# Weights as one hi/lo buffer at three offsets, and four operand arrangements in the FFN's way up

## The chip, the cores and the metric

The kernel runs on one core of one Trainium2 chip. The metric is device time in microseconds (us). The kernel before took 1268.47 us, the median of 3 runs (1268.17 to 1268.96). TensorE does the matmuls, ScalarE (ACT) and VectorE (DVE) the elementwise work, and DMA queues bring the weights in.

## The reference

A causal decoder trunk of two layers on 512 tokens of width 1024, all in float32. Cut to what matters:

```python
x = x + even_mixer(rmsnorm(x, norm_mix[0]), ...)   # gated linear attention + differential attention
x = x + conv_ffn(rmsnorm(x, norm_ffn[0]), ...)
x = x + odd_mixer(rmsnorm(x, norm_mix[1]), ...)    # three groups of dilated windowed attention
x = x + conv_ffn(rmsnorm(x, norm_ffn[1]), ...)

def conv_ffn(h, w_up, conv_w, conv_b, w_down):     # w_up: 1024 x 5632, w_down: 2816 x 1024
    u = causal_depthwise_conv3(h @ w_up, conv_w) + conv_b
    gate, val = jnp.split(u, 2, axis=-1)
    return (jax.nn.silu(gate) * val) @ w_down
```

## The kernel before

The residual `xT` stays on chip, features on the partitions and the 512 tokens along the free axis, in 8 chunks of 128 features. Every dense product takes float32r operands. Each float32 operand is split as `hi` + `lo`, and a product is three matmuls: hi*hi, lo*hi and hi*lo, added in one PSUM bank of 512 float32 columns. A matmul has a stationary operand (128x128, brought in by its own LDWEIGHTS) and a moving operand, whose columns stream past it.

**Weights.** `weight_slabs()` lists 208 pieces ("slabs") in the order of their use. Most are 128 x 1024 values, 8 row chunks of 128 columns in the FFN's way up. `load_next()` (lines 160 to 176) brings one in: a DMA from SyncE's queue into `raw`, an ACT copy that rounds it into `hi` (line 171), and a DVE subtraction that leaves `lo` (line 174). `raw`, `hi` and `lo` are tiles of 1088 elements (4352 bytes) on each partition with 3 copies each, so slab i uses copy i mod 3. `slab()` hands out slab i and first issues the loads up to slab i+2, so the slab being converted is used two slabs later and goes into the copy that slab i-1 has just left.

**Products.** `tok_gemm` (line 304) is for the mixers' input projections: the tokens `hhi`/`hlo` are stationary and the weights move. For the second and third attention group of layer 1 the 128 stationary tokens are every fourth one (`v1`, line 793), so that an LDWEIGHTS reads every fourth float32 of a row. `feat_gemm` (line 320) is for the mixers' output projections: weights stationary, activations moving. The FFN works on 22 hidden chunks in groups of 8, 8 and 6. `up(j)` (lines 700 to 708) computes one 128-feature chunk of the way up: 8 row chunks times 3 matmuls, weights stationary, all 512 tokens of `hhi`/`hlo` moving, into one bank. It runs for the gate half and the value half of each chunk, 44 times in each layer. `gate` (line 724) does the convolution, SiLU and product on DVE and ACT and splits the result into `ghi`/`glo`. `down` (line 740) is the way down: weights stationary, `ghi`/`glo` moving (line 747).

**Order.** TensorE runs in the order in which the code emits its work. In the mixers small attention products are put between the dense ones at estimated times. The FFN is emitted straight, way up and way down by groups, and the first chunk of the next group's way up goes ahead of a way down. The other engines are scheduled by the framework, which puts a wait where tiles are reused.

Of the kernel before, what the change touches and what calls it, by code (L numbers as in the profile page):

```python
"""Two-layer hybrid trunk (GLA + differential attention, dilated attention, conv-FFN) on one core.

The residual stays on chip feature-major.  Every dense product runs on TensorE with float32r operands: each
float32 operand w is split exactly as w = hi + lo (hi rounded to float32r, lo the rest) and the product is
hi*hi + hi*lo + lo*hi in float32 PSUM.  The attention products are plain float32.
"""
# [11 lines left out]
F32R = mybir.dt.float32r  # L18
# [6 lines left out]
P = 128  # L25
S = 512
D = 1024
# [7 lines left out]
# columns of the packed constant array  # L35
C_ID, C_LT, C_SM = 0, P, 2 * P
C_KEEP = C_SM + 8
# the rest is kept only as long as it is needed
# [29 lines left out]
# groups of the FFN's hidden chunks that stay on chip between the way up and the way down  # L68
# [3 lines left out]

def weight_slabs():
    """The weights' pieces in the order of their use: (array, layer, first row, chunks of 128 rows, first column,
    columns).  On chip a piece has a row of each chunk on every partition."""
    slabs = []

    def tok(w, c0, n):
        nk = 2 if n == 512 else 4
        slabs.extend((w, 0, k * P, nk, c0, n) for k in range(0, DC, nk))  # L80

    def ffn(i):
        for gi, (f0, n) in enumerate(GROUPS):
            # the next group's first chunk goes before this group's way down
            for j in range(f0 + (gi > 0), f0 + n + (gi < 2)):
                slabs.extend(("ffn_w_up", i, 0, DC, half + j * P, P) for half in (0, DFF))
            slabs.extend(("ffn_w_down", i, f0 * P, n, c * P, P) for c in range(DC))

    for c0, n in ((2576, 512), (1552, 512), (2064, 512), (0, 512), (1280, 272), (512, 512), (1024, 256)):
        tok("ev_w_in", c0, n)  # L90
    for r0 in (512, 0):
        slabs.extend(("ev_w_out", 0, r0, 4, c0, 256) for c0 in range(0, D, 256))
    ffn(0)
    for g, kind in ((0, 0), (0, 1), (1, 0), (1, 1), (2, 0), (2, 1), (1, 2), (2, 2), (0, 2)):
        tok("od_w_in", g * 1536 + kind * 512, 512)
    slabs.extend(("od_w_out", 0, 0, 4, c0, 256) for c0 in range(0, D, 256))
    ffn(1)
    return slabs


def lay_out(a):
    """The kernel's arrays: the inputs in the order in which the chip reads them."""
    def cols(v):
        """(..., 128 n) with 128 consecutive entries on the partitions."""
# [5 lines left out]
    weights = [a[w][i, r0:r0 + nk * P, c0:c0 + n].reshape(nk, P, n).transpose(1, 0, 2).ravel()  # L110
               for w, i, r0, nk, c0, n in weight_slabs()]
# [11 lines left out]
def trunk_kernel(ctx: ExitStack, tc: tile.TileContext, x, weights, params, lqks, w_a2, consts, out):  # L123
# [18 lines left out]
    # ---------------------------------------------------------------- constants and small parameters  # L142
# [7 lines left out]
    # ---------------------------------------------------------------- weight slabs  # L150
# [3 lines left out]
    for _, _, _, a, _, b in weight_slabs():  # L154
        slabs.append((weights[off:off + P * a * b].rearrange("(p n) -> p n", p=P), a, b))
        off += P * a * b

    loaded = []

    def load_next():  # L160
        src, a, b = slabs[len(loaded)]
        n = a * b
        raw = wp.tile([P, SLAB], F32, name="raw", bufs=3)
        hi = wp.tile([P, SLAB], F32R, name="hi", bufs=3)
        lo = wp.tile([P, SLAB], F32R, name="lo", bufs=3)
        # the first product waits for its weights: they come in halves
# [8 lines left out]
        v = [t[:, :n].rearrange("p (a b) -> p a b", a=a) for t in (hi, lo)]  # L175
        loaded.append(v)

# [9 lines left out]
    # ---------------------------------------------------------------- residual, h, norms  # L187
# [4 lines left out]
    def split(hi, lo, src, gain):  # L192
        """hi + lo = src * gain, each in float32r."""
# [7 lines left out]
    def rsqrt(dst, ss, scale, work=None):  # L201
        """dst = 1 / sqrt(ss * scale + EPS): a table start and a Newton step."""
# [23 lines left out]
    def rstd_of(cols):  # L226
        """1/rms of tokens, one column of 128 tokens for each entry of cols (views of sqacc)."""
# [8 lines left out]
    def rstd_rows():  # L236
        """1/rms of tokens as a row for every partition."""
# [17 lines left out]
    def masked(out, sc, mask, nm):  # L255
        """out = -(sc + mask), nm its row minimum: minus the row maximum of the masked scores."""
# [3 lines left out]
    # ---------------------------------------------------------------- TensorE's order  # L260
    # TensorE runs in emission order in the mixers.  The dense products are the background; a piece of attention
    # work is put into the stream once its estimated time has come, so that it finds its operands ready.
# [28 lines left out]
    def tok_gemm(n, lhs, evict, before=None):  # L291
        """Token-major projection block: n columns, lhs(h, t) the stationary tokens."""
# [20 lines left out]
    def feat_gemm(nk, ncol, rhi, rlo, evict):  # L313
        """Feature-major product: one slab of nk row chunks and ncol columns, moving rhi/rlo[k]."""
# [13 lines left out]
    # ================================================================ layer 0 mixer  # L328
# [3 lines left out]
    def norm_scale(src, nh, r=None):  # L332
        """1/rms of each of nh heads of src along the free axis; r scales src's rows first."""
# [20 lines left out]
    def qk_evict(dst, gain, nh, r, tag, then=None):  # L354
        """Normalise heads, lay them feature-major into dst."""
# [29 lines left out]
    with tc.tile_pool(name="m0", bufs=1) as m0, tc.tile_pool(name="t0", bufs=2) as t0:  # L385
# [18 lines left out]
        def prepare_params():  # L404
            """Parameters that the first products do not need."""
            # gains that enter scores: both norms' gains and the score scale on the query side
# [12 lines left out]
        # ---- start: a slab of weights for every two chunks of the residual  # L419
# [32 lines left out]
        def head_norm(src, n, dst_hi, dst_lo, gain, gate, tag):  # L452
            """RMS-norm each 128-wide head of src (SBUF, token-major), gate, and lay it feature-major as hi + lo."""
# [10 lines left out]
        # ---- differential attention, one (query tile, head) after the other  # L464
        # estimated waits, in us
# [60 lines left out]
        # ---- gated linear attention, one 128-token tile after the other  # L526
# [38 lines left out]
        def decay3(t, y2):  # L565
            """exp of a tile's summed decays and of its first chunk's, by head, the 64 rows twice."""
# [59 lines left out]
        def when_landed(fn):  # L626
            """After the values and all gates have been produced."""
# [47 lines left out]
        def late(t, ps):  # L675
            # the residual's norm is known only by then
# [20 lines left out]
    # ================================================================ FFN  # L697
    def ffn(i, done):
        with tc.tile_pool(name=f"f{i}", bufs=2) as fp:
            def up(j):  # L700
                whi, wlo = slab()
                ps = bank()
                for kc in range(DC):
                    for m, (w, r) in enumerate(((whi, hhi), (wlo, hhi), (whi, hlo))):
                        T.matmul(ps, w[:, kc], r[:, kc], start=(kc == 0 and m == 0),  # L705
# [34 lines left out]
            def down(gi):  # L740
# [15 lines left out]
                # the last group's last chunk comes late: it enters four accumulators after all the others  # L756
# [9 lines left out]
                for c in range(first, DC):  # L766
                    w = slab()
                    # the kernel's last chunk goes out in halves
# [23 lines left out]
    # ================================================================ layer 1 mixer  # L792
# [3 lines left out]
    # groups 1 and 2 take their tokens by residue modulo 4; dilation 16 is a mask within a residue's tile  # L796
# [11 lines left out]
    with tc.tile_pool(name="m1", bufs=1) as m1:  # L808
# [8 lines left out]
        # probabilities: a block of 128 keys for each (head, query tile)  # L817
# [168 lines left out]
```

## Time and profile before

| | before |
|---|---|
| median of 3 runs | 1268.47 us |
| span of the profiled execution | 1266.7 us |
| PE busy | 1254.2 us (99%) |
| DVE busy | 766.1 us (60%) |
| ACT busy | 541.2 us (43%) |
| weights and inputs read | 110.37 MB |

The profiled execution is one run of the program. Its own time is its span, from the first to the last instruction; the median of the timed runs is 1.8 us longer than that span. PE is TensorE's matmul side and PEld its weight loads, which overlap the matmuls. A matmul's record is longer (about 0.39 us) than the distance to the next matmul's start, since they are pipelined; the pace of a stream is read from the starts, or from the chain of work that ended last, which counts each piece of time once.

### The profile page before, as it was taken

How to read it: one execution, taken by the hardware profiler on the slowest of the kernel's cores; microseconds unless marked ns; L12 is line 12 of the kernel's file. 1: busy time of each engine (PE TensorE's matmuls, PEld its weight loads, DVE VectorE, ACT ScalarE, POOL GpSimd, SP SyncE). 2: the span in 40 equal slices, each digit the busy share in tenths (PEclk: the TensorE clock that was granted, in tenths of full speed). 3: DMA queues.
4: the chain of work that ended last, by engine and by line, in shares of the span. 5: the costliest groups of instructions: out<-in, count | busy, mean ns of one | idle time of the engine just before them, and what ended most of it. 6: DMA issues, size and time to landing. Idle time of an engine off the chain costs nothing.

```text
span 1266.7 us, 15144 instructions
## 1 busy us (share of the span) xinstructions
PE 1254.2 (99%) x5878; PEld 1053.7 (83%) x5878; DVE 766.1 (60%) x1409; ACT 541.2 (43%) x895; POOL 5.7 (0%) x13
## 2 busy tenths in 40 slices
PE   8999999999999999999999999999999999999998
PEld 6878688888888888888889999988888888888887
DVE  6457769777753775377545554363787636773573
ACT  5446555444432443145435554435454324442341
POOL 0000000000000000000000000000000000000000
PEclk9999999999999999999999999999999999999999
DMA  7222121233223223322322222231233323322322
GB/s 248 84 85 68 34 68 34 84 101 100 87 97 100 97 89 98 100 91 75 124 84 72 79 67 93 76 90 45 84 100 100 93 91 100 100 89 94 100 75 92
DMA packets 33783, 113.49 MB, mean 90 GB/s; under 512 B 3943, under 2 KB 4744, under 8 KB 33712
## 3 DMA queue, kind: packets, MB, share of 16 engines
q1 hardware_dynamic: 32256, 110.32, 27.9%
q10 hardware_dynamic: 1296, 2.10, 0.4%
q8 instruction: 46, 0.75, 0.2%
q14 instruction: 25, 0.20, 0.1%
q0 software_dynamic: 160, 0.12, 0.0%
HBM read 110.37 MB, written 2.15 MB: 89 GB/s over the span
## 4 chain that ended last, share of the span: by engine, by line
PE 97%; DVE 1%; ACT 1%; DMA 0%; issue 0%; SPq 0%; ACTq 0%
PE bank L705 38%; PE bank L304 27%; PE bank L747 19%; PE bank L320 5%; PE bank L350 1%; PE bank L918 1%; PE bank L478 1%; PE bank L512 1%; PE bank L850 1%; PE bank L906 0%; PE bank L839 0%; PE bank L500 0%; DMA xT<-in_xT_dram 0%; PE bank L231 0%; PE bank L569 0%; PE bank L616 0%
## 5 line engine op out<-in xcount | busy, mean ns | idle before, releaser
L171 ACT ACTIVATE hi<-raw 128x1024 fp32r<-128x1024 f32 (+2 forms) x209 | 217.0, 1039 | 337.3 <-PE bank L747 152.4
L174 DVE TENSOR_TENSOR lo<-raw,hi 128x1024 fp32r<-128x1024 f32 (+2 forms) x209 | 250.6, 1200 | 167.0 <-ACT hi L171 163.3
L705 PE MATMUL bank<-hhi,hi 128*128 128x512 f32 x704 | 277.4, 394 | 0.0
L705 PE MATMUL bank<-hhi,lo 128*128 128x512 f32 x704 | 275.7, 392 | 0.0
L705 PE MATMUL bank<-hlo,hi 128*128 128x512 f32 x704 | 274.4, 390 | 0.0
L304 PE MATMUL bank<-hi,hhi 128*128 128x512 f32 (+2 forms) x512 | 207.3, 405 | 6.0 <-ACT hi L171 5.6
L304 PE MATMUL bank<-hi,hlo 128*128 128x512 f32 (+2 forms) x512 | 197.1, 385 | 0.0
L304 PE MATMUL bank<-lo,hhi 128*128 128x512 f32 (+2 forms) x512 | 196.8, 384 | 0.0
L705 PEld LDWEIGHTS bank<-hlo,hi 128*128 128x128 f32 x704 | 132.2, 188 | 30.1
L705 PEld LDWEIGHTS bank<-hhi,hi 128*128 128x128 f32 x704 | 132.2, 188 | 29.5 <-issue 0.5
L705 PEld LDWEIGHTS bank<-hhi,lo 128*128 128x128 f32 x704 | 132.3, 188 | 28.1 <-issue 0.5
L747 PE MATMUL bank<-glo,hi 128*128 128x512 f32 (+1 forms) x358 | 139.9, 391 | 0.0
L747 PE MATMUL bank<-ghi,lo 128*128 128x512 f32 (+1 forms) x358 | 139.9, 391 | 0.0
L747 PE MATMUL bank<-ghi,hi 128*128 128x512 f32 (+1 forms) x358 | 139.9, 391 | 0.0
L304 PEld LDWEIGHTS bank<-hi,hhi 128*128 128x128 f32 x512 | 120.3, 235 | 18.0 <-ACT hi L171 5.6
L304 PEld LDWEIGHTS bank<-lo,hhi 128*128 128x128 f32 x512 | 120.1, 235 | 11.9 <-DVE lo L174 0.2
L304 PEld LDWEIGHTS bank<-hi,hlo 128*128 128x128 f32 x512 | 121.0, 236 | 10.6 <-DVE hlo L199 0.5
L752 DVE TENSOR_TENSOR xT<-xT,bank 128x512 f32<-128x512 f32 (+1 forms) x49 | 33.2, 677 | 115.3 <-PE bank L747 115.3
L747 PEld LDWEIGHTS bank<-ghi,lo 128*128 128x128 f32 x358 | 67.4, 188 | 15.3
L747 PEld LDWEIGHTS bank<-ghi,hi 128*128 128x128 f32 x358 | 67.5, 188 | 15.2
L747 PEld LDWEIGHTS bank<-glo,hi 128*128 128x128 f32 x358 | 67.5, 188 | 15.2
L195 ACT ACTIVATE ghi<-cv 128x512 fp32r<-128x512 f32 x44 | 27.7, 630 | 109.4 <-DVE cv L730 109.4
(193 smaller groups left out, 1283.1 us busy)
## 6 DMA issues: line engine op xcount, KB each, us to landing
raw<-in_weights_dram SPq DMA_DIRECT2D x189, 512.0 KB, 3.5
raw<-in_weights_dram SPq DMA_DIRECT2D x16, 384.0 KB, 3.0
xT<-in_xT_dram SPq DMA_DIRECT2D x8, 256.0 KB, 5.4
out_dram<-xT ACTq DMA_DIRECT2D x7, 256.0 KB, 2.1
raw<-in_weights_dram SPq DMA_DIRECT2D x2, 544.0 KB, 3.6
raw<-in_weights_dram SPq DMA_DIRECT2D x2, 256.0 KB, 3.4
tr<-in_consts_dram SPq DMA_DIRECT2D x1, 256.0 KB, 4.3
wide<-in_consts_dram SPq DMA_DIRECT2D x1, 256.0 KB, 5.4
```

Of the source, the lines that this page charges most:

```text
L171: r = A.activation(hi[:, c0:c1], raw[:, c0:c1], AF.Copy)
L174: V.tensor_tensor(out=lo[:, c0:c1], in0=raw[:, c0:c1], in1=hi.bitcast(F32)[:, c0:c1], op=ALU.subtract)
L195: A.activation(hi, src, AF.Copy)
L304: T.matmul(ps[t][:, :n], lhs(a[:, kc], t), b[:, k, :n], start=(kc == 0 and j == 0), stop=(kc == DC - 1 and j == 2))
L320: T.matmul(ps, w[:, k, d * P:(d + 1) * P], r(k), start=(k == 0 and j == 0), stop=(k == nk - 1 and j == 2))
L350: T.transpose(pt[:, h * P:(h + 1) * P], src[:, h * P:(h + 1) * P], ident)
L478: T.matmul(sc[:, :nk], qT[rs, h, n * P:(n + 1) * P], kT[rs, h, :nk], start=True, stop=True)
L512: T.matmul(po[n][:, h * P:(h + 1) * P], wT[:, j * P:(j + 1) * P], bv[:, j, h * P:(h + 1) * P], start=(h == 0 and j == 0), stop=(h == 3 and ...
L705: T.matmul(ps, w[:, kc], r[:, kc], start=(kc == 0 and m == 0), stop=(kc == DC - 1 and m == 2))
L747: T.matmul(ps[:, ts], a[:, k], b[f0 + k][:, ts], start=(k == 0 and m == 0), stop=(k == n - 1 and m == 2))
L752: V.tensor_tensor(out=xT[:, c, ts], in0=xT[:, c, ts], in1=ps[:, ts], op=ALU.add)
L850: T.matmul(sc[:, hs], q[:, h, ts], k[:, h, ts], start=(h == 0), stop=(h == 3))
```

## The change

`hi` and `lo` come to lie in one tile `hl` of 2 x 1088 + 24 elements (8800 bytes) on each partition, with 3 copies; `lo` begins 1088 elements after `hi`, as far as one `hi` copy lay from the next before. Copies of `hi` were 4352 bytes apart, 17 times 256; they come to lie 8800 bytes apart, 96 more than 34 times 256. Tiles that are placed behind the weights move by 288 bytes.

Each slab has two flags. `alt` interleaves hi and lo element by element, so that ACT writes, DVE reads and writes, and LDWEIGHTS reads with a step of 8 bytes. `fall` reverses the token order: the moving operand is read from token 511 down to 0, and the bank is written in the same reversed order, so that each token's column stays at its place. Slabs outside the way up have both flags off. In the way up `home_forms` gives three slabs to each of the four combinations in turn: of the 88 slabs 24 have neither flag, 22 `fall` alone, 21 `alt` alone and 21 both. The number and order of all instructions, the amounts moved and the arithmetic stay as they were.

```diff
+def home_forms():
+    n = 0
+    while True:
+        yield ((False, False), (True, False), (False, True), (True, True))[n // 3 % 4]
+        n += 1
...
             for j in range(f0 + (gi > 0), f0 + n + (gi < 2)):
-                slabs.extend(("ffn_w_up", i, 0, DC, half + j * P, P) for half in (0, DFF))
+                slabs.extend(("ffn_w_up", i, 0, DC, half + j * P, P, next(form)) for half in (0, DFF))
...
     def load_next():
-        src, a, b = slabs[len(loaded)]
+        src, a, b, (fall, alt) = slabs[len(loaded)]
         n = a * b
         raw = wp.tile([P, SLAB], F32, name="raw", bufs=3)
-        hi = wp.tile([P, SLAB], F32R, name="hi", bufs=3)
-        lo = wp.tile([P, SLAB], F32R, name="lo", bufs=3)
+        hl = wp.tile([P, 2 * SLAB + 24], F32R, name="hl", bufs=3)
+        if alt:
+            hi, lo = (hl[:, :2 * n].rearrange("p (n u) -> p u n", u=2)[:, u] for u in range(2))
+        else:
+            hi, lo = hl[:, :n], hl[:, SLAB:SLAB + n]
...
-        v = [t[:, :n].rearrange("p (a b) -> p a b", a=a) for t in (hi, lo)]
+        v = [t.rearrange("p (a b) -> p a b", a=a) for t in (hi, lo)]
         loaded.append(v)
+        falls.append(fall)
...
             def up(j):
                 whi, wlo = slab()
+                way = slice(None, None, -1 if falls[used[0] - 1] else 1)
                 ps = bank()
                 for kc in range(DC):
                     for m, (w, r) in enumerate(((whi, hhi), (wlo, hhi), (whi, hlo))):
-                        T.matmul(ps, w[:, kc], r[:, kc], start=(kc == 0 and m == 0),
+                        T.matmul(ps[:, way], w[:, kc], r[:, kc, way], start=(kc == 0 and m == 0),
                                  stop=(kc == DC - 1 and m == 2))
```

## Rows read from the trace of the kernel before

**Rows 1.** The page's head: the span, and busy time, share of the span and instructions of each engine; then the view of the cores, with the mean granted TensorE clock.

```profile
span 1266.7 us, 15144 instructions
PE 1254.2 (99%) x5878; PEld 1053.7 (83%) x5878; DVE 766.1 (60%) x1409; ACT 541.2 (43%) x895; POOL 5.7 (0%) x13
...
core 0: 1266.7 us, clock 1.000
```

**Rows 2.** The chain of work that ended last: its shares by line, and some of its long pieces in order of time. Columns: start us, length us, what, number of matmuls.

```profile
by line: PE bank L705 38.2%; PE bank L304 27.0%; PE bank L747 19.4%; PE bank L320 4.9%; PE bank L350 1.5%; PE bank L918 1.0%; PE bank L478 0.8%; PE bank L512 0.6%; PE bank L850 0.6%; PE bank L906 0.5%; PE bank L839 0.5%; PE bank L500 0.4%; 
...
65.37 16.80 PE bank L304 x72
...
355.30 44.62 PE bank L747 x192
399.93 87.91 PE bank L705 x384
...
239.90 15.63 PE bank L320 x67
...
705.01 1.73 PE bank L839 x8
```

**Rows 3.** Matmul groups by line and shape: count, busy us and mean ns of one record, idle time ahead. Line 705 is the way up, 304 the input projections, 747 the way down.

```profile
L705 PE MATMUL bank<-hhi,hi 128*128 128x512 f32 x704 | 277.4, 394 | 0.0
L705 PE MATMUL bank<-hhi,lo 128*128 128x512 f32 x704 | 275.7, 392 | 0.0
L705 PE MATMUL bank<-hlo,hi 128*128 128x512 f32 x704 | 274.4, 390 | 0.0
L304 PE MATMUL bank<-hi,hhi 128*128 128x512 f32 x448 | 188.4, 421 | 6.0 <-ACT hi L171 5.6 <-ACT hhi L198 0.4
L747 PE MATMUL bank<-ghi,hi 128*128 128x512 f32 x346 | 136.5, 394 | 0.0
```

**Rows 4.** Timeline of TensorE in the way up: the first matmul of four slabs in a row, 24 matmuls from one to the next. Columns: start us, length us, engine, line, operation.

```profile
405.28 0.39 PE L705 MATMUL bank<-hhi,hi 128*128 128x512 f32 x1
...
410.77 0.39 PE L705 MATMUL bank<-hhi,hi 128*128 128x512 f32 x1
...
416.26 0.39 PE L705 MATMUL bank<-hhi,hi 128*128 128x512 f32 x1
...
421.76 0.39 PE L705 MATMUL bank<-hhi,hi 128*128 128x512 f32 x1
```

**Rows 5.** Timeline of an output projection of layer 1 (line 320): two matmuls with 66 starts from the first to the second.

```profile
882.38 0.39 PE L320 MATMUL bank<-o1lo,hi 128*128 128x512 f32 x1
...
897.34 0.39 PE L320 MATMUL bank<-o1lo,hi 128*128 128x512 f32 x1
```

**Rows 6.** Timeline of an input projection of layer 1 whose stationary tokens are every fourth one: two matmuls with 45 starts from the first to the second, and between them one that starts together with the next weight load. Then the same in the way up, where the load's operand is contiguous.

```profile
711.01 0.40 PE L304 MATMUL bank<-lo,hhi 128*128 128x512 f32 x1
...
711.97 0.40 PE L304 MATMUL bank<-hi,hhi 128*128 128x512 f32 x1
711.97 0.31 PEld L304 LDWEIGHTS bank<-hi,hlo 128*128 128x128 f32 x1
...
721.73 0.40 PE L304 MATMUL bank<-lo,hhi 128*128 128x512 f32 x1
...
405.51 0.39 PE L705 MATMUL bank<-hhi,lo 128*128 128x512 f32 x1
405.51 0.19 PEld L705 LDWEIGHTS bank<-hlo,hi 128*128 128x128 f32 x1
```

**Rows 7.** Timeline of ACT and DVE as a slab is converted in the way up.

```profile
405.48 1.06 ACT L171 ACTIVATE hi<-raw 128x1024 fp32r<-128x1024 f32 x1 [4.45 <-PE bank L705]
...
406.57 1.23 DVE L174 TENSOR_TENSOR lo<-raw,hi 128x1024 fp32r<-128x1024 f32 x1 [0.40 <-ACT hi L171]
```

**Rows 8.** Two ACT copies of 128x512 from a bank: line 365 writes contiguous runs, line 928 writes every fourth float32. Columns: duration ns min/median/max, first and last start.

```profile
L365 ACT ACTIVATE k<-bank x12: 581/597/599, 673.5 to 791.1; 128x512 f32<-128x512 f32 x12
...
L928 ACT ACTIVATE oacc<-bank x4: 1090/1094/1118, 854.6 to 866.9; 128x512 f32<-128x512 f32 x4
```

**Rows 9.** Busy time by engine in 33 us of the way up (six slabs) with the granted TensorE clock, DMA share and GB/s; then that of line 171 and of line 174 alone in the same stretch.

```profile
405.00:438.00 33.00, 33.00 (x145) 27.05 (x145) 23.27 (x29) 14.45 (x18) 0.00 (x0) 1.00 0.30 97
...
405.00:438.00 33.00, 6.37 (x6) 1.00 0.30 97
...
405.00:438.00 33.00, 7.36 (x6) 1.00 0.30 97
```

**Rows 10.** The only wait of TensorE for weights, in the view of who waited for whom: total us, times, longest. Then two rows of the first microseconds: a matmul that starts on the first chunk of `hhi` while later chunks of the same tile are still to be written.

```profile
PE bank L304 <- ACT hi L171: 5.6, 1, 5.6
...
5.61 0.80 PE L304 MATMUL bank<-hi,hhi 128*128 128x512 f32 x1 [5.61 <-ACT hi L171]
...
6.89 0.72 ACT L198 ACTIVATE hhi<-xT,prm 128x512 fp32r<-128x512 f32 x1 [0.57 <-DMA xT<-in_xT_dram]
```

More of the change, by code (lines that the diff above doesn't have):

```diff
@@ L70 @@
 LEAD = 2
+def home_forms():
[3 more added lines that the diff above has]
+        n += 1
 def weight_slabs():
     slabs = []
+    form = home_forms()
     def tok(w, c0, n):
         nk = 2 if n == 512 else 4
-        slabs.extend((w, 0, k * P, nk, c0, n) for k in range(0, DC, nk))
+        slabs.extend((w, 0, k * P, nk, c0, n, (False, False)) for k in range(0, DC, nk))
     def ffn(i):
@@ L85, in ffn @@
             for j in range(f0 + (gi > 0), f0 + n + (gi < 2)):
-                slabs.extend(("ffn_w_up", i, 0, DC, half + j * P, P) for half in (0, DFF))
-            slabs.extend(("ffn_w_down", i, f0 * P, n, c * P, P) for c in range(DC))
+                slabs.extend(("ffn_w_up", i, 0, DC, half + j * P, P, next(form)) for half in (0, DFF))
+            slabs.extend(("ffn_w_down", i, f0 * P, n, c * P, P, (False, False)) for c in range(DC))
     for c0, n in ((2576, 512), (1552, 512), (2064, 512), (0, 512), (1280, 272), (512, 512), (1024, 256)):
@@ L91, in weight_slabs @@
     for r0 in (512, 0):
-        slabs.extend(("ev_w_out", 0, r0, 4, c0, 256) for c0 in range(0, D, 256))
+        slabs.extend(("ev_w_out", 0, r0, 4, c0, 256, (False, False)) for c0 in range(0, D, 256))
     ffn(0)
@@ L95, in weight_slabs @@
         tok("od_w_in", g * 1536 + kind * 512, 512)
-    slabs.extend(("od_w_out", 0, 0, 4, c0, 256) for c0 in range(0, D, 256))
+    slabs.extend(("od_w_out", 0, 0, 4, c0, 256, (False, False)) for c0 in range(0, D, 256))
     ffn(1)
@@ L109, in lay_out @@
     conv = np.concatenate([a["ffn_conv_w"][:, :, 0], a["ffn_conv_b"][:, None]], axis=1)
-    weights = [a[w][i, r0:r0 + nk * P, c0:c0 + n].reshape(nk, P, n).transpose(1, 0, 2).ravel()
-               for w, i, r0, nk, c0, n in weight_slabs()]
+    weights = [a[w][i, r0:r0 + nk * P, c0:c0 + n].reshape(nk, P, n)
+               .transpose(1, 0, 2).ravel()
+               for w, i, r0, nk, c0, n, _ in weight_slabs()]
     return {
@@ L153, in trunk_kernel @@
     off = 0
-    for _, _, _, a, _, b in weight_slabs():
-        slabs.append((weights[off:off + P * a * b].rearrange("(p n) -> p n", p=P), a, b))
+    for _, _, _, a, _, b, form in weight_slabs():
+        slabs.append((weights[off:off + P * a * b].rearrange("(p n) -> p n", p=P), a, b, form))
         off += P * a * b
     loaded = []
+    falls = []
     def load_next():
-        src, a, b = slabs[len(loaded)]
+        src, a, b, (fall, alt) = slabs[len(loaded)]
         n = a * b
         raw = wp.tile([P, SLAB], F32, name="raw", bufs=3)
-        hi = wp.tile([P, SLAB], F32R, name="hi", bufs=3)
-        lo = wp.tile([P, SLAB], F32R, name="lo", bufs=3)
+        hl = wp.tile([P, 2 * SLAB + 24], F32R, name="hl", bufs=3)
[3 more added lines that the diff above has]
+            hi, lo = hl[:, :n], hl[:, SLAB:SLAB + n]
         cut = n if loaded else n // 2
```

## The prediction

> **What bounds the kernel now.** I read the page's head first: PE is busy 99% of the span, DVE 60% and ACT 43% [rows 1]. A busy PE can still wait inside, so the chain of waits comes next. It is TensorE nearly throughout: the way up (line 705) 38.2%, the input projections 27.0%, the way down 19.4% [rows 2], and TensorE waits for weights once, at the start [rows 10]. No transfer and no other engine is late. The change adds and removes no instruction, so that the question is how far apart two matmuls start, and whether a conversion can become late.
>
> The pace is read from the pieces of the chain. All these streams have one shape (128x128 stationary, 512 columns moving) and run at a granted clock of 1.000, the 2.4 GHz level [rows 1, 9], at which 512 columns last 213.3 ns. Yet they differ: the way up 87.91/384 = 228.9 ns, the way down 44.62/192 = 232.4, an input projection 16.80/72 = 233.3, an output projection of layer 0 15.63/67 = 233.3 [rows 2], one of layer 1 14.96/66 = 226.7 [rows 5]. Plain float32 matmuls, which come as two records of 256 columns in two passes, start every 1.73/8 = 216.3 ns [rows 2]. So some 10 to 17 ns of each float32r matmul depend on which operands meet. In the way up that is 12.6 ns times 2112 matmuls (3 x 704, [rows 3]), 27 us in all: the most that this stage holds in its pace, unless it beats the float32 row.
>
> Does the place of the weights matter? Before, the three copies gave the same pace: 5.49, 5.49 and 5.50 us for three slabs in turn [rows 4]. But those copies lie a multiple of 256 bytes apart, and their lo parts too; the trace holds no shift of 32, 64 or 96 bytes, while streams over other tiles have other paces. I take the pace to depend on low address bits of the two operands, which the change alters.
>
> **The change part by part.** *Conversions.* Each slab still takes one ACT copy and one DVE subtraction, 1.06 and 1.23 us [rows 7]. In the 42 interleaved slabs both write at a step of 8 bytes. The nearest row is an ACT copy that writes at 16 bytes, 1094 ns against 597, a factor of 1.83 [rows 8]; the other end is no change. At 1.83 a slab costs ACT 0.88 and DVE 1.02 us more. Six slabs in a row are interleaved, and over six slabs DVE has 23.27 of 33.00 us busy, 7.36 in these subtractions, and ACT 14.45, 6.37 in these copies [rows 9]. They would rise to 29.4 and 19.7 us, which still fits. Nor is it late: the copy that starts at 405.48 ends as lo at 407.80 [rows 7] and its slab is the third of rows 4 and starts at 416.26, 8.5 us later. Queued behind it are the gate's steps of the same chunk, with 29.4 of 33 us done in time. I charge 0. If that cover were gone, each of 42 slabs could lay up to 1.9 us on TensorE, 80 us; nothing speaks for it.
>
> *One tile for hi and lo.* A copy is now free when both halves are: one matmul, 0.23 us, later at most, against 8.5 us of slack, so 0. At the very start the first matmul could have to wait for lo as well as for hi if waits went by whole tiles, but a matmul starts on one chunk of hhi at 5.61 while another is written at 6.89 [rows 10], so they go by region: 0, at the most 1.4 us (two half subtractions).
>
> *Interleaved weight loads*, 42 x 24 = 1008 matmuls. A load at a step of 16 bytes takes 0.31 us instead of 0.19, and its matmuls start 10.72/45 = 238.2 ns apart [rows 6], 4.9 more than the same line with contiguous tokens (233.3). So even a load longer than the pace costs little. The ends: 226.7 (-2.2 us) and 238.2 (+9.4 us). A step of 8 lies between the contiguous row and the 16-byte row; I take +2 ns, 2.0 us.
>
> By the Trainium skill (Advanced Engine Details and Errata, section Memory Cachelines) SBUF lines have 16 bytes, and two hits on a line suffice to hide its latency; a 16-byte step of float32 has one, an 8-byte step two. By that rule the interleaved loads would stay at the contiguous duration and this term would be 0, the sum 1267.0. The 0.31 us row agrees for one hit; no row shows two.
>
> *Reversed tokens*, 43 x 24 = 1032 matmuls, both the moving read and the bank's write. No row shows a matmul operand at a negative step. Below, the float32 pace of 216.3 gives -12.6 ns, -13.0 us. Above, if the stream loses what the strided ACT write loses, 228.9 x 1.83 gives 419 ns, +190 ns, +196 us. The ends are far apart; a reversed run touches the same neighbouring bytes as a forward one, unlike the strided rows, so it is nearest to the contiguous row, and I take 0.
>
> *Offsets.* The paces of the four contiguous kinds average (226.7 + 228.9 + 232.4 + 233.3)/4 = 230.3. If new offsets draw from these, the way up loses 1.4 x 2112 = 3.0 us, the way down gains 2.1 x 1038 = 2.2 [rows 3], and the contiguous input projections, 768 of the 1344 matmuls (six of fourteen wide projections are strided), gain 3.0 x 768 = 2.3. The sum is -1.5 us. The ends: all at 226.7, -4.6 - 5.9 - 5.1 = -15.6 us; all at 233.3, +9.3 + 0.9 = +10.2 us.
>
> The sum: 0 + 0 + 2.0 + 0 - 1.5 = +0.5 us on a span of 1266.7, so 1267.2; with the 1.8 us by which the median of the runs exceeds that span, 1269.0 us.
>
> **The rivals.** *Gain: the new arrangements part the two reads.* The moving stream and the next weight load start within 10 ns of each other and run side by side [rows 6]; if their order sets the 10 to 17 ns, a shift or a reversal may remove part. For it: the paces differ though the shape doesn't. Against: the way up is already near the low end. With every offset at 226.7 (-15.6) the time is 1252.9; with the reversed half at 216.3 besides (-10.4 x 1032 = -10.7) it is 1242. I take 1255.
>
> *Slower: reversed streams lose their pairing.* Place: the 1032 reversed matmuls. Price: +196 us as above, 1465 us; even 3 ns more for each would be slower by over 0.2%. For it: strided accesses cost 1.6 to 1.8 times in this trace [rows 6, 8]. Against: they skip bytes, and a reversal doesn't. It decides from the point at which a reversed matmul's step exceeds 231.4 ns (2.5 us over 1032).
>
> The Trainium skill (same page and section) says of PSUM that its lines hold two float32 and that any non-contiguous pattern significantly slows matmuls. By a strict reading a negative step is such a pattern; the page gives no factor, and no row here shows one.
>
> *Slower by a little: the way up drifts to the slow paces.* Interleaved matmuls at 238.2 (+9.4) and the other 1104 at 233.3 (+4.9) give 1282.8. For it: the stage is near the best pace now, so most draws are worse. Against: way down and projections draw too, from the slow end.
>
> *The change doesn't do what it says:* the pace belongs to the stage and not to addresses, as equal copies suggest [rows 4]. Then offsets give 0 and 1268.5 to 1270.5 remains, within the forecast.
>
> **How the numbers follow.** A difference under about 0.2%, 2.5 us, can't be told from none. The forecast, with its own range 1262 to 1275, gets 0.40, of which 0.09 is faster, 0.21 the same and 0.10 slower. The gain gets 0.26, the drift 0.16, the slow reversal 0.18. So faster 0.35, same 0.21, slower 0.44. The range leaves out the slow reversal and little else: 1246, some way into the gain's lower end, to 1290, past the drift's 1282.8.
>
> **What would show it.** The pieces of the chain in the way up, divided by their matmuls, for each of the four arrangements and three copies: contiguous ones within 226 to 234 ns, interleaved ones up to 238, reversed ones like their forward twins. LDWEIGHTS of interleaved slabs: 0.19 (two hits suffice) or towards 0.31. ACT's line of the hi copy and DVE's of the lo subtraction at up to 1.94 and 2.25 us in interleaved slabs, with no wait of TensorE on them. Way down and input projections off 232.4 and 233.3 by some ns, differently by copy; if they stay, offsets don't matter. I am wrong if the reversed slabs run above 240 ns, if any arrangement falls to about 216, or if TensorE starts to wait for hi or lo.

## The result and the profile after

The changed kernel takes 1277.36 us (median of 3 runs, 1276.60 to 1278.25) against 1268.47 us: 1.0071 times the time before, with an interval of 1.0051 to 1.0091. It is slower by 8.9 us. The span of the profiled execution grew from 1266.7 to 1274.8 us, by 8.1 us.

The page's head and the view of the cores, to be read beside [rows 1]:

```profile
span 1274.8 us, 15128 instructions
PE 1262.3 (99%) x5878; PEld 1061.2 (83%) x5878; DVE 761.3 (60%) x1409; ACT 541.9 (43%) x895; POOL 5.6 (0%) x13
...
core 0: 1274.8 us, clock 1.000
```

PE grew by 8.1 us, as much as the span, with the same 5878 matmuls at the same granted clock of 1.000. DVE and ACT hardly moved. The 16 instructions fewer are semaphore instructions (5 on VectorE, 7 on ScalarE, 4 on TensorE); those that do work are as many as before. So the matmuls stand further apart. The chain of work that ended last tells which (columns as in [rows 2]; line 722 is the way up, 320 the input projections, 764 the way down, 336 the output projections):

```profile
65.21 16.76 PE bank L320 x72
...
267.87 89.40 PE bank L722 x384
357.27 44.56 PE bank L764 x192
401.83 89.42 PE bank L722 x384
```

The way up went from 87.91 us for 384 matmuls [rows 2] to 89.40, from 228.9 to 232.8 ns each. Over 2112 matmuls that is 3.9 x 2112 = 8.2 us, as much as the whole loss. The way down is at 44.56/192 = 232.1 ns (before 232.4), the first long input projection at 16.76/72 = 232.8 (before 233.3). Adding the steps from one matmul's start to the next over each whole stage agrees:

```
us, from the starts     before   after
way up                   484.3   492.4
way down                 241.2   240.9
input projections        329.6   328.7
output projections        68.8    69.3
```

TensorE's wait for weights stayed the one at the start. The view of who waited for whom:

```profile
PE bank L320 <- ACT hl L186: 5.8, 1, 5.8
```

The next three answers are those for line 722, line 186 (the ACT copy) and line 189 (the DVE subtraction); durations are in ns, min/median/max, then first and last start. A weight load in the way up lasts 187 to 200 ns (187 to 193 where contiguous, 192 to 200 where interleaved), far from the 0.31 us of a 16-byte step [rows 6]. The ACT copy's longest is 1.19 us; contiguous ones of 1024 elements are at 1.06 in the median. The DVE subtraction kept its 1.23 us; its longest, 1.29, is that of 1088 elements.

```profile
L722 PEld LDWEIGHTS bank<-hhi,hl x1408: 187/189/200, 255.5 to 1237.0; 128*128 128x128 f32 x176
...
L186 ACT ACTIVATE hl<-raw x209: 630/1061/1192, 5.1 to 1258.9; 128x1024 fp32r<-128x1024 f32 x95, 128x768 fp32r<-128x768 f32 x8, 128x512 fp32r<-128x512 f32 x1, 128x1088 fp32r<-128x1088 f32 x1
...
L189 DVE TENSOR_TENSOR hl<-raw,hl x209: 692/1226/1294, 5.8 to 1259.7; 128x1024 fp32r<-128x1024 f32 x95, 128x768 fp32r<-128x768 f32 x8, 128x512 fp32r<-128x512 f32 x1, 128x1088 fp32r<-128x1088 f32 x1
```

Last, the timeline in the way up, to be read like [rows 4]: the third matmul of twelve slabs in a row, 24 matmuls from one row to the next. From the first row on, three slabs are interleaved, three both interleaved and reversed, three have neither flag, and three are reversed. Each group goes through the copies of `hl` in the order 2, 0, 1.

```profile
290.56 0.39 PE L722 MATMUL bank<-hlo,hl 128*128 128x512 f32 x1
...
296.14 0.40 PE L722 MATMUL bank<-hlo,hl 128*128 128x512 f32 x1
...
301.73 0.40 PE L722 MATMUL bank<-hlo,hl 128*128 128x512 f32 x1
...
307.30 0.40 PE L722 MATMUL bank<-hlo,hl 128*128 128x512 f32 x1
...
312.90 0.40 PE L722 MATMUL bank<-hlo,hl 128*128 128x512 f32 x1
...
318.50 0.40 PE L722 MATMUL bank<-hlo,hl 128*128 128x512 f32 x1
...
324.10 0.39 PE L722 MATMUL bank<-hlo,hl 128*128 128x512 f32 x1
...
329.68 0.39 PE L722 MATMUL bank<-hlo,hl 128*128 128x512 f32 x1
...
335.20 0.39 PE L722 MATMUL bank<-hlo,hl 128*128 128x512 f32 x1
...
340.77 0.40 PE L722 MATMUL bank<-hlo,hl 128*128 128x512 f32 x1
...
346.37 0.40 PE L722 MATMUL bank<-hlo,hl 128*128 128x512 f32 x1
...
351.97 0.40 PE L722 MATMUL bank<-hlo,hl 128*128 128x512 f32 x1
```

Interleaved 5.58, 5.59, 5.57 us; both 5.60, 5.60, 5.60; neither 5.58, 5.52, 5.57; reversed 5.60, 5.60. Before, every slab took 5.49 or 5.50. Only slabs with neither flag in copy 0 still come near that. Over all 88 slabs, the mean step by arrangement and copy is, in ns:

```
                    copy 0   copy 1   copy 2
neither              229.1    232.6    233.3
reversed             233.4    234.5    233.3
interleaved          233.5    231.5    232.1
both                 233.3    233.3    233.3
```

Against 228.9 ns, the neither slabs (576 matmuls) lose 1.6 us, the reversed (528) 2.6, the interleaved (504) 1.7 and both (504) 2.2, 8.1 us in all. Every arrangement loses something, and all entries but one (234.5) lie between 229.1 and 233.5. What belongs to the offsets and what to the arrangements, this table can't say.

### The profile page after: what moved, and what is told of

Read it like the earlier page. It is cut to its first block, busy times and chain, and to the rows that moved or that the text cites. A ratio compares the mean times of both kernels' runs of the same rounds, so it can differ in the third digit from the quotient of the medians.

```text
span 1274.8 us, 15128 instructions
## 1 busy us (share of the span) xinstructions
PE 1262.3 (99%) x5878; PEld 1061.2 (83%) x5878; DVE 761.3 (60%) x1409; ACT 541.9 (43%) x895; POOL 5.6 (0%) x13
## 4 chain that ended last, share of the span: by engine, by line
PE 98%; ACT 1%; DVE 0%; DMA 0%; issue 0%; SPq 0%
PE bank L722 39%; PE bank L320 27%; PE bank L764 19%; PE bank L336 5%; PE bank L366 2%; PE bank L935 1%; PE bank L494 1%; PE bank L528 1%; PE bank L867 1%; PE bank L923 0%; PE bank L856 0%; PE bank L516 0%; DMA xT<-in_xT_dram 0%; PE bank L632 0%; PE bank L247 0%; PE bank L585 0%
## 5 line engine op out<-in xcount | busy, mean ns | idle before, releaser
L722 PE MATMUL bank<-hhi,hl 128*128 128x512 f32 x1408 | 443.3, 396 | 0.0
L186 ACT ACTIVATE hl<-raw 128x1024 fp32r<-128x1024 f32 (+2 forms) x209 | 220.8, 1057 | 343.1 <-PE bank L764 151.8
L189 DVE TENSOR_TENSOR hl<-raw,hl 128x1024 fp32r<-128x1024 f32 (+2 forms) x209 | 250.6, 1200 | 183.0 <-ACT hl L186 168.3
L320 PE MATMUL bank<-hl,hhi 128*128 128x512 f32 (+2 forms) x1024 | 331.2, 395 | 5.9 <-ACT hl L186 5.8
L722 PEld LDWEIGHTS bank<-hhi,hl 128*128 128x128 f32 x1408 | 269.4, 191 | 59.1 <-issue 1.0
L722 PE MATMUL bank<-hlo,hl 128*128 128x512 f32 x704 | 278.6, 396 | 0.0
L320 PEld LDWEIGHTS bank<-hl,hhi 128*128 128x128 f32 x1024 | 225.5, 235 | 29.3 <-ACT hl L186 5.8
L764 PE MATMUL bank<-ghi,hl 128*128 128x512 f32 (+1 forms) x716 | 221.0, 390 | 0.0
L320 PE MATMUL bank<-hl,hlo 128*128 128x512 f32 (+2 forms) x512 | 197.2, 385 | 0.0
L764 PE MATMUL bank<-glo,hl 128*128 128x512 f32 (+1 forms) x358 | 140.1, 391 | 0.0
```

Source lines behind the costliest of these rows:

```text
L186: r = A.activation(hi[:, c0:c1], raw[:, c0:c1], AF.Copy)
L189: V.tensor_tensor(out=lo[:, c0:c1], in0=raw[:, c0:c1], in1=hi.bitcast(F32)[:, c0:c1], op=ALU.subtract)
L320: T.matmul(ps[t][:, :n], lhs(a[:, kc], t), b[:, k, :n], start=(kc == 0 and j == 0), stop=(kc == DC - 1 and j == 2))
L722: T.matmul(ps[:, way], w[:, kc], r[:, kc, way], start=(kc == 0 and m == 0), stop=(kc == DC - 1 and m == 2))
L764: T.matmul(ps[:, ts], a[:, k], b[f0 + k][:, ts], start=(k == 0 and m == 0), stop=(k == n - 1 and m == 2))
```

## Experiments

All kernels but `e10_halves` compute what the two kernels compute, with as many matmuls. "Before" is the kernel before, on the same chip in the same session. Where one execution is compared, the profile's spans and steps carry the argument.

**Offsets alone.** The changed kernel with both flags off everywhere (`e1_offsets`):

```diff
-        yield ((False, False), (True, False), (False, True), (True, True))[n // 3 % 4]
+        yield (False, False)
```

> The changed kernel with both flags off in every slab: only the shared buffer and its three offsets are left. Theory A (the pace follows from where the stationary weights lie against the moving operand): forward slabs keep the paces that the changed kernel's own forward slabs show by copy, about 229.1, 232.6 and 233.3 ns, mean 231.6, so the way up costs 2.7 ns x 2112 = 5.7 us more than before and the span is about 1272.4 us. Rival B (it is the switching of arrangements that costs, the offsets don't): 228.9 ns in every copy, span about 1266.7 us.

Measured: 1275.34 us, before 1270.32, span 1273.6. The chain:

```profile
268.41 89.08 PE bank L722 x384
357.48 44.66 PE bank L764 x192
402.14 89.02 PE bank L722 x384
```

The way up's 384 matmuls take 89.05 us, 231.9 ns each: 228.9 in copy 0, 232.7 in copy 1, 233.3 in copy 2. That is 490.5 us in the stage, +6.2. Offsets alone cost three quarters of the loss. So the pace belongs to addresses, not to the stage.

**Arrangements alone.** The changed kernel without the 24 elements of padding, so that the copies lie a multiple of 256 bytes apart again (`e2_forms`):

```diff
-        hl = wp.tile([P, 2 * SLAB + 24], F32R, name="hl", bufs=3)
+        hl = wp.tile([P, 2 * SLAB], F32R, name="hl", bufs=3)
```

> The changed kernel without the 24 added elements, so that its copies lie a multiple of 256 bytes apart as before, and the four arrangements in turn. Theory A: forward contiguous slabs at 228.9 ns in all copies, reversed ones at about 233.4, interleaved ones at 231.5 to 233.5, so (22 x 4.5 + 21 x 3.4 + 21 x 4.4) x 24 = 6.3 us more than before, span about 1273. Rival: reversal and interleaving cost only through the offsets: all slabs at 228.9, span about 1266.7.

Measured: 1275.75 us, span 1274.0. The timeline, third matmul of slabs in a row (one with both flags, three with neither, one reversed):

```profile
318.33 0.40 PE L722 MATMUL bank<-hlo,hl 128*128 128x512 f32 x1
...
323.92 0.40 PE L722 MATMUL bank<-hlo,hl 128*128 128x512 f32 x1
...
329.43 0.39 PE L722 MATMUL bank<-hlo,hl 128*128 128x512 f32 x1
...
334.92 0.39 PE L722 MATMUL bank<-hlo,hl 128*128 128x512 f32 x1
...
340.43 0.40 PE L722 MATMUL bank<-hlo,hl 128*128 128x512 f32 x1
...
346.02 0.40 PE L722 MATMUL bank<-hlo,hl 128*128 128x512 f32 x1
```

5.59 with both flags, then 5.51, 5.49, 5.51 with neither, then 5.59 reversed. Every slab with any flag runs at 233.3 to 233.4 ns in every copy, the others at 229.05. The way up takes 491.2 us, +6.9. Each part alone costs most of the loss, then, and they don't add: 6.2 + 6.9 = 13.1 us apart, 8.1 together. What brings a stream to 233.3 ns costs nothing more in one that is there already.

**The pace against the offset.** The kernel before, with `hi` and `lo` starting 0, 16, ... 240 bytes into their tiles by the slab's number (`e3_scan16`):

```diff
+        if n <= SLAB - 64:
+            o = 4 * (len(loaded) % 16)
+            hi, lo = hi[:, o:o + n], lo[:, o:o + n]
```

> The kernel before, with hi and lo of each slab (all but those of 272 columns) starting 0, 16, 32, ... 240 bytes into their tiles in turn; nothing else moves. Theory A: the pace of the way up depends on this offset with steps of some ns between about 226.7 and 233.3 ns: 228.9 at 0, about 232.6 at 96, 233.3 at 192, perhaps 226.7 at 64, where the distance to the moving operand is that of the 226.7 ns output projection. Rival C (the alignment of the weights alone, to 64 bytes, sets it): 0, 64, 128 and 192 alike at 228.9. Rival D (the pace belongs to the stage): 228.9 throughout.

Measured: 1274.32 us, span 1272.5. Four slabs in a row, at offsets 64, 80, 96 and 112:

```profile
279.06 0.40 PE L708 MATMUL bank<-hhi,hi 128*128 128x512 f32 x1
...
284.52 0.39 PE L708 MATMUL bank<-hhi,hi 128*128 128x512 f32 x1
...
289.97 0.39 PE L708 MATMUL bank<-hhi,hi 128*128 128x512 f32 x1
...
295.56 0.40 PE L708 MATMUL bank<-hhi,hi 128*128 128x512 f32 x1
...
301.16 0.39 PE L708 MATMUL bank<-hhi,hi 128*128 128x512 f32 x1
```

5.46 and 5.45 us, then 5.59 and 5.60: sixteen bytes more and each matmul starts 6 ns later. All sixteen (ns):

```
offset       0    16    32    48    64    80    96   112   128   144   160   176   192   208   224   240
way up   228.9 233.3 233.4 227.3 226.8 226.7 233.4 233.3 233.2 232.1 234.3 233.3 233.3 233.5 233.1 230.0
way down 233.5 233.5 233.3 230.0 228.9 233.3 233.5 226.8 226.7 226.7 233.1 233.3 233.2 232.1 234.3 233.3
```

The way down has the curve of the way up, shifted by 64 bytes. By the placement of the tiles in the kernel before (worked out from their sizes; no row shows an address), `hhi` lies 64 bytes and `ghi` 128 bytes beyond the weights, counted modulo 256. So both stages are quickest, 226.7 to 227.3 ns, where the moving operand and the weights start at the same address modulo 256, within 16 bytes. With the places that the change gives its copies (0, 96 and 192 modulo 256 from the first, and 32 for `ghi`), this curve gives 228.9, 233.4 and 233.3 for the way up and 234.3, 228.9 and 233.1 for the way down. The changed kernel's slabs with neither flag ran at 229.1, 233.3 and 232.6, its way down at 234.3, 229.1 and 233.3, if copy 0 lies at the first of these places, copy 2 at the second and copy 1 at the third. That order is inferred: with copies 1 and 2 the other way round the way down would not fit.

**Distance or alignment.** In the kernel before, one small tile ahead of everything made 96 bytes longer, so that all operands move together (`e4_shift`):

```diff
-    cst = per.tile([P, C_KEEP], F32, name="cst")
+    cst = per.tile([P, C_KEEP + 24], F32, name="cst")
...
-            L.dma_start(cst, consts[:, :C_KEEP])
+            L.dma_start(cst[:, :C_KEEP], consts[:, :C_KEEP])
```

> The kernel before with one small tile ahead of all others made 96 bytes longer, so that moving and stationary operands all move by 96 bytes and keep their distances. Theory A (distance): the paces stay, 228.9, 232.4, 233.3 ns, span 1266.7. Rival C (alignment of an operand by itself): the paces of several stages change by some ns, as they do in the changed kernel, where copies moved by 96 and 192 bytes.

Measured: 1271.66 us, span 1269.9. The chain:

```profile
269.06 87.91 PE bank L705 x384
356.97 44.62 PE bank L747 x192
```

Both are those of [rows 2] to 0.01 us, and copies agree. A move of both operands by 96 bytes changes nothing, so the pace follows their distance and not an alignment of their own. The 3.2 us by which the span is longer lie in the input projections (333.0 us against 329.6), at the lower clock level; the last section comes back to it.

**The other arrangements against the offset.** The changed kernel without padding; all of layer 0's way up interleaved, all of layer 1's reversed, each over sixteen offsets (`e5_scans`):

```diff
-        yield ((False, False), (True, False), (False, True), (True, True))[n // 3 % 4]
+        yield (False, True) if n < 44 else (True, False)
...
+        o = 4 * turn[len(loaded)]
...
```

> The shared buffer without the 24 added elements. In the way up of layer 0 all slabs are interleaved, in that of layer 1 all are reversed, and in both hi and lo start 0, 16, ... 240 bytes into their copy in turn; the slabs of the second mixer's input projection also take 16 offsets. Theory A (the moving read and the next weight load run into each other where their addresses meet, and the distance decides): forward contiguous weights had a window of 48 to 80 bytes at 226.7 ns; a reversed stream meets the load head-on at any distance, so its pace hardly depends on the offset, 233 to 234 ns throughout; an interleaved load walks through its addresses as fast as the moving stream, so its pace depends on the offset, with at least one window below 229. Rival E (an arrangement has its own fixed price): 233.3 ns at every offset in both.

Measured: 1277.43 us, span 1275.6, way up 492.8 us. Reversed: 233.3 at fourteen offsets, 236.7 at 208 and 240; the offset can only do harm. Interleaved: 230.0 (at 128 and 176) to 233.6; the quick window that was expected there is missing. An interleaved slab has no good place among these sixteen, and no fixed price either, as rival E had it. (By its own duration an interleaved load covers 1024 bytes of a partition in some 0.195 us, while the moving stream covers 2048 in about 0.23: it doesn't walk as fast as the stream, as the theory assumed.)

**Which half of the reversal costs.** The kernel of `e3_scan16`; layer 0 reverses the moving read alone, layer 1 the bank's write alone (`e10_halves`):

```diff
-                        T.matmul(ps, w[:, kc], r[:, kc], start=(kc == 0 and m == 0),
+                        T.matmul(ps[:, ::-1] if i else ps, w[:, kc], r[:, kc] if i else r[:, kc, ::-1],
+                                 start=(kc == 0 and m == 0),
...
```

> The kernel before with the offsets of the scan over all slabs (hi and lo start 0, 16, ... 240 bytes into their tiles by the slab's number), and the reversal cut in two: in layer 0's way up only the moving read is reversed, in layer 1's only the write to the bank. The tokens' order in the bank is then reversed and the output isn't the reference's; no work is left out. Theory A (the reversal costs by the meeting of the moving read with the weight load): the reversed read gives a flat 233.3 ns at every offset as with both reversed, and the reversed write alone gives the forward curve unchanged (228.9 at 0, 226.7 at 64, 233.3 at 128). Theory B (a bank written backwards is what costs): the reversed write is flat at 233.3 and the reversed read follows the forward curve.

Measured: 1275.39 us, before 1269.23, span 1273.6. Offsets 64, 80 and 96, first with the read reversed, then with the write:

```profile
279.60 0.40 PE L708 MATMUL bank<-hhi,hi 128*128 128x512 f32 x1
...
285.20 0.40 PE L708 MATMUL bank<-hhi,hi 128*128 128x512 f32 x1
...
290.80 0.40 PE L708 MATMUL bank<-hhi,hi 128*128 128x512 f32 x1
...
296.40 0.40 PE L708 MATMUL bank<-hhi,hi 128*128 128x512 f32 x1
...
947.61 0.39 PE L708 MATMUL bank<-hhi,hi 128*128 128x512 f32 x1
...
953.05 0.39 PE L708 MATMUL bank<-hhi,hi 128*128 128x512 f32 x1
...
958.50 0.39 PE L708 MATMUL bank<-hhi,hi 128*128 128x512 f32 x1
...
964.09 0.40 PE L708 MATMUL bank<-hhi,hi 128*128 128x512 f32 x1
```

5.60, 5.60, 5.60 against 5.44, 5.45, 5.59. The write alone follows the forward curve at all sixteen offsets within 0.2 ns; the read alone is at 233.3 to 233.4 in twelve and at 234.9 to 236.7 in the others (48, 192, 208, 240), and never gets near 227. The bank written backwards costs nothing; the price is that of the read, and theory B falls. That the reversed read costs by meeting the weight load, as theory A has it, is argued and not shown: a fixed price of the reversed read itself wasn't tried apart from the loads. That four offsets cost more than the others speaks for the meeting.

**Hi and lo apart.** The kernel before, with separate offsets for `hi` and `lo` in the FFN, eight by eight (`e7_two`; `turn` holds the two offsets of each slab, in steps of 32 bytes):

```diff
...
+        oh, ol = turn[len(loaded)]
+        hi, lo = hi[:, oh:oh + n], lo[:, ol:ol + n]
```

> The kernel before with separate offsets of hi (0, 32, ... 224 bytes, changing with every slab) and lo (the same eight, changing every eight slabs) in the way up and the way down. Two of three weight loads fetch hi, one lo. Theory A, load by load: each load has its own price by its own distance, so hi at 64 with lo elsewhere stays within 2 to 3 ns of 226.7 and lo at 64 with hi elsewhere is near 231; both at 64 the best. If one distance decides alone, the other offset has no effect.

Measured: 1275.38 us, span 1273.6, way up 490.9 us, way down 240.9. With `hi` at 64 and `lo` elsewhere the way up is at 231 to 233, not within 3 ns of 226.7; most of the 64 pairs are at 230 to 234. The gain doesn't come load by load: both halves have to be at the home distance. A miss for the additive form of the theory. (One pair, 64 and 64, gave 228.2 here where `e3_scan16` gave 226.8; the slabs beside it had other offsets.)

**Everything at the home distance.** The kernel before, with offsets of 64 bytes in the way up and the 512- and 256-column projections, 128 in the way down and layer 0's output projections, 0 elsewhere (`e6_home`):

```diff
+    home = [{"ffn_w_up": 16, "ffn_w_down": 32, "ev_w_out": 32, "od_w_out": 0}.get(w, 16 if b != 272 else 0)
+            for w, _, _, _, _, b in weight_slabs()]
...
+        o = home[len(loaded)]
+        hi, lo = hi[:, o:o + n], lo[:, o:o + n]
```

> The kernel before with hi and lo shifted inside their tiles by 64 bytes in the way up and the input projections, by 128 in the way down and the first mixer's output projection, 0 in the second's: the offsets at which moving and stationary operand lie a multiple of 256 bytes apart. Theory A: 226.7 ns in the way up (-2.2 x 2112 = -4.6 us), in the way down (-5.7 x 1038 = -5.9) and in the output projection of layer 0 (-6 x 192 = -1.2), and about 228 in the contiguous input projections (-5 x 768 = -3.8): some 15 us less than before, ratio about 0.988. Rival D (what the scan showed comes from turning offsets between slabs): no gain.

Measured: 1254.85 us (4 runs, 1254.00 to 1255.45) against 1268.85 (7 runs): 0.9886 times, interval 0.9869 to 0.9902, span 1253.7. The chain:

```profile
65.30 16.35 PE bank L308 x72
...
265.87 87.08 PE bank L709 x384
352.95 43.56 PE bank L751 x192
```

All three now run at one pace: 227.1, 226.8 and 226.9 ns, where [rows 2] gave 233.3, 228.9 and 232.4. By stage: way up 479.7 us (-4.6), way down 235.5 (-5.7), output projections 67.9 (-0.9), input projections 327.4 (-2.2). It beats the kernel before by 14.0 us, and so the changed one too, with the same instructions. The place of the weights is all that differs; that it counts by its distance from the other operand rests on `e4_shift` above and `e9_tokens` below. Rival D falls.

**Another place for the strided projections** (`e8_home2`), which still ran at 235.0 in `e6_home`: 152 bytes, where their curve in `e3_scan16` was lowest.

```diff
+            if w != "od_w_in" or c0 < 1536 else 38
```

> The kernel with weights at their home offsets (e6_home), but 152 in place of 64 bytes for the six input projections whose stationary tokens are every fourth one, for which the scans showed 233.3 ns at 144 and 160 and 234.6 to 235.0 at 64. Theory A: 1.5 ns x 576 = 0.9 us less than e6_home, so some 15 us less than the kernel before, ratio about 0.988; the other stages stay at 226.7 to 228.

Measured: 1256.74 us (1256.09 to 1257.29) against 1270.70, ratio 0.9896 (0.9879 to 0.9912), the same as `e6_home` within the intervals. The strided projections took 238.7 ns, not 233.3. A miss: the turning scan, where neighbouring slabs had other offsets, doesn't carry over to one constant offset there.

**The same distance by moving the tokens.** The kernel before, with the weights where they were and `hhi` and `hlo` moved by 192 bytes (`e9_tokens`; what lies behind them moves by 256):

```diff
+    front = per.tile([P, 48], F32, name="front")
     xT = per.tile([P, DC, S], F32, name="xT")
...
+    back = per.tile([P, 16], F32, name="back")
+    V.memset(front[:, 0:1], 0.0)
+    V.memset(back[:, 0:1], 0.0)
```

> The kernel before with the normed tokens hhi and hlo moved by 192 bytes and every tile behind them by 256, so that weights, ghi and glo keep their places among each other to 256 bytes, and no weight offset, order or form is changed. Theory A (distance between moving and stationary operand): the way up falls to 226.7 ns (-4.6 us) and the contiguous input projections, in which hhi is stationary, to about 227 (-4.8 us), the strided ones to about 235 (-1.7 us); the way down stays at 232.4; span about 1255.6. Rival C (the place of the weights): nothing changes, 1266.7.

Measured: 1262.73 us, before 1270.70, span 1261.0. The chain:

```profile
266.65 87.08 PE bank L709 x384
353.73 44.79 PE bank L751 x192
```

The way up runs at 226.8 ns with not one weight byte moved, so it is the distance, from either side. The way down, whose operands both moved by 256 bytes and kept their distance, went from 232.4 to 233.3 ns, +1.0 us, which no theory expected: the distance doesn't settle the last nanosecond. The rest of the miss against the expected span lies in the input projections (327.2 us), as in `e6_home`.

## Why the prediction was right or wrong

The time, 1277.36 us, is inside 1246 to 1290 and on the side that held the largest chance, slower; the likeliest single case, 1269.0 and no change that can be told, didn't come. That the time is inside is in part luck: it lies above the forecast's own range of 1262 to 1275, and the range around it was drawn wide for the rivals. The sum missed on both sides: the way up lost 8.2 us where its terms gave 5.0, and the gains set against it, 2.2 and 2.3 us, came to 0.3 and 0.9. Step by step:

- *What bounds the kernel.* Right: the question was the distance of matmul starts, and TensorE took the whole change in its own pace.
- *Conversions, 0 us.* Right. The interleaved ACT copy grew by 12% at most (1061 to 1192 ns), not by 83%, the DVE subtraction not at all, and TensorE waited for no weights but the first.
- *One tile for hi and lo, 0 us.* Right: the first wait is 5.8 us after 5.6 [rows 10].
- *Interleaved loads, +2.0 us.* Too small by the pace: 4.4 ns in `e2_forms`, not 2, so 4.4 x 1008 = 4.4 us alone. The loads themselves stayed at 187 to 200 ns. On that, the Trainium skill's rule (Advanced Engine Details and Errata, section Memory Cachelines) that two hits on a 16-byte line suffice agrees with the trace to some 7 ns (192 to 200 against 187 to 193); the sum of 1267.0 that went with it didn't come, because the pace rose though the loads hardly grew. The load's length doesn't tell the pace, and the 2 ns that I took were a choice between the ends without a row for this step.
- *Reversed tokens, 0 us.* Wrong. "Nearest to the contiguous row" was the failed choice: 233.3 ns instead of 228.9, 4.4 x 1032 = 4.5 us alone (`e2_forms`), and the slabs with this flag lose 4.8 us of the 8.1 in the changed kernel (2.6, and 2.2 in those that are also interleaved). Neighbouring bytes don't help: `e10_halves` puts all of the cost on the moving read and none on the write. How the read comes by it isn't shown.
- *Offsets, -1.5 us.* The mechanism was right, the size not. The way up lost 6.2 us alone (`e1_offsets`) instead of 3.0; the way down gained 0.3 instead of 2.2; the input projections 0.9 instead of 2.3. The four paces seen in the trace were taken for a fair sample with a mean of 230.3. The sixteen offsets of `e3_scan16` average 231.6, and ten of them lie at 233 or above: the sample was kinder than the curve.
- *The sum.* The terms for the way up added to +5.0 us (3.0 + 2.0 + 0) where 8.2 came. Alone, each part costs more still (13.1 us together), but most slabs that leave 228.9 end near 233.3 whatever took them there, which the sum over parts didn't foresee.

Of the rivals, *drift to the slow paces* is what happened, at a little over half its price (8.1 of 14.3 us): interleaved slabs went to 231.5 to 233.5, not 238.2. Its price rested on a 16-byte step's row. The *slow reversal* got past the point from which it decides (231.4 ns), but by 2 ns and not 190, far from the factor of 1.83 that was its price. The Trainium skill's rule (Advanced Engine Details and Errata, section Memory Cachelines) that a non-contiguous PSUM pattern significantly slows matmuls has no price here, if a step of -1 counts as such a pattern: the backwards write alone kept 226.7 ns at offset 64. The *gain* was there to be had, not by parting the reads but by the opposite, giving them the same address modulo 256; the change's offsets missed that place in every copy. *The pace belongs to the stage* falls with `e1_offsets`.

## What to carry over

Where a stream of matmuls starts further apart than its columns last, and no wait shows, compare the paces of streams of one shape and scan the offset of one operand against the other over 256 bytes. Here the same address modulo 256 for the weights and the moving operand was worth 1.1% of the whole kernel, at no instruction. Price a change of layout by the paces that a scan gives, not by the length of the load or the copy, and don't count on such costs to add: here 6.2 and 6.9 us alone were 8.1 together.

## What the hardware showed that I had not expected

The pace of a float32r matmul with 512 columns depends on where the weights lie relative to the moving operand: 226.7 to 227.3 ns within 16 bytes of the same place modulo 256, and up to 234.3 elsewhere; in the strided projections up to 238.7. The Trainium skill (SBUF — State Buffer, section Who interferes with whom) gives TensorE two SBUF read ports, one for the moving operand and one for weight loads, and calls them independent. In their effect on the pace they aren't here: moving the weights alone (`e6_home`) or the tokens alone (`e9_tokens`) changes the pace, moving both (`e4_shift`) doesn't. How they meet inside isn't shown, nor why 226.7 remains above the 216.3 of plain float32 [rows 2].

Open: why the way down took 232.4 ns in one kernel and 233.3 in `e9_tokens` at the same distance; why `hi` and `lo` both have to be at home; and a fall of the clock. In `e6_home` TensorE's granted clock falls at the start of layer 1's projections; in the profiled execution of the kernel before, in the stretch of the same work, it doesn't (windows of 4 us; the columns are those of [rows 9], the granted clock the third from the right). First `e6_home`, then before:

```profile
624.00:628.00 4.00, 4.00 (x23) 3.77 (x23) 0.20 (x2) 1.06 (x2) 0.00 (x0) 1.00 0.18 75
628.00:632.00 4.00, 4.00 (x13) 3.15 (x12) 1.52 (x4) 0.42 (x2) 0.00 (x0) 0.62 0.43 125
```

```profile
632.00:636.00 4.00, 4.00 (x23) 3.77 (x22) 1.26 (x3) 1.38 (x3) 0.00 (x0) 1.00 0.00 0
636.00:640.00 4.00, 4.00 (x18) 3.20 (x17) 0.46 (x4) 0.00 (x0) 0.00 (x0) 1.00 0.46 134
```

0.62 is a stretch partly at the 1.2 GHz level: 13 matmuls against 18. Some ten matmuls start about 0.43 us apart there, which costs about 2 us, and with about 1 us more at the lower level in the first projection it takes back part of what the input projections gained by their pace. PE counts as busy just before, in both kernels, but what it runs there are sixteen matmuls of one column each (the timeline; first `e6_home`, then before):

```profile
624.95 2.81 PE L235 MATMUL bank<-cst,sqacc 128*128 128x1 f32 x16
```

```profile
631.89 2.81 PE L231 MATMUL bank<-cst,sqacc 128*128 128x1 f32 x16
```

These sixteen stand there in all twelve profiled executions. In six of them (`e3_scan16`, `e4_shift`, `e5_scans`, `e6_home`, `e8_home2`, `e9_tokens`) the clock falls shortly after, in the other six it doesn't. In `e4_shift` (0.59 in 636 to 640 us) the paces are those of before, so the quicker pace isn't needed for it. Nor does a change of the kernel seem to be: of the 14 executions of the kernel before that were timed beside `e6_home` and `e9_tokens`, six with a mean granted clock of 1.000 took 1268.23 to 1268.51 us, and eight with 0.998 or 0.999 took 1268.85 to 1271.13. Where in those the clock fell isn't recorded, and what brings the fall wasn't tried.
